# Early modulation sums and Hyena products moved to VectorE, the value transform folded modulo 4, and weight splits placed when both engines are empty

## The chip, the cores and the metric

The kernel runs on one core of a Trainium2 chip. The metric is the time of one execution on the device, in microseconds (us). In the text PE is TensorE, DVE is VectorE, ACT is ScalarE, POOL is GpSimd, and SP is the sync engine, whose queue issues nearly all transfers.

## What is computed

One inference step of a two-layer diffusion backbone for 512 latent tokens and 128 context tokens of width 1024 (640 columns in all). Layer 0 mixes attention and a long convolution (Hyena), layer 1 is a bidirectional mLSTM; after each comes a gated feed-forward part. Every part is shifted, scaled and gated by a modulation vector, once for the latents (`c`) and once for the context (`c_ctx`). The parts that the change touches:

```python
mod_p = jnp.split(silu(c_ctx) @ w_mod[l] + b_mod[l], 6, axis=-1)
mod_s = [m[:, None, :] for m in jnp.split(silu(c) @ w_mod[l] + b_mod[l], 6, axis=-1)]

def long_conv(v, h):                 # n = 2 L
    V = jnp.fft.rfft(v, n=n, axis=1)
    Hf = jnp.fft.rfft(h, n=n, axis=0)
    return jnp.fft.irfft(V * Hf[None], n=n, axis=1)[:, :L]

# Hyena: u -> x0, x1, v after a width-3 convolution
v = v * x1
y = long_conv(v, h_f) + flip(long_conv(flip(v), h_b)) + skip * v
return y * x0

# after each mixer
xp = xp + mod_p[2] * rms_norm(out_p, norm_mix_post[l])
xs = xs + mod_s[2] * rms_norm(out_s, norm_mix_post[l])
```

## The kernel before

**Products.** Weights come from memory in tiles of 128x1024 (512 KB, `wr`). Each is split into a rounded high part `wh` (an ACT cast) and a low part `wl` (a DVE subtraction), and so are the activations (`a0h`, `a0l`). A product is then the sum of three: high by high, high by low, low by high. The Hyena transforms and transposes run in plain fp32; each such matmul leaves two records in the trace, a transpose one.

**Order of the work.** A planner (`Order`) writes the program. It keeps an estimated clock for each engine. The main tasks are PE's, in a fixed sequence. Everything else (evacuations, modulation sections, the Hyena chain, attention) is a *side*: a generator that is stepped when its time has come by PE's clock (`pump`, lines 187 to 201). A side with a lead may start when DVE's and ACT's queues stand no more than that lead ahead of PE; one spawned with a slack is held to that slack instead. When no side is due and both queues are short, `pump` calls `idle`, which splits the next weights. PE executes in the order written, and so does every other engine: an instruction that waits holds up all behind it on its engine.

**A modulation section** (`mod_section`, one of six per layer, named by layer and number) multiplies 1024 rows of `w_mod` by the two vectors, in eight steps over tiles `mw` of 128x1024, of which two are resident. At each step the sum for the latents, `acc[0]`, is one DVE instruction (SCALAR_TENSOR_TENSOR). For the context ACT multiplies into `modp` and POOL adds it to `acc[1]`. Then PE sums over the partitions (`finish`): for sections (0,3) and (0,4) with one-column products `modt`, for the gate section (0,2) with products `modp` of `onesr` and the two parts of a split (`moda`, `modb`), whose result DVE multiplies by a gain row `modn` and stores in a row `gate`. Sections (0,3) and (0,4) run in the projection of layer 0. Section (0,2) is spawned with a slack once the four convolution outputs (keys `("y", i)`) are there; it lies around the start of attention, and its gates are needed by the first post-norm (`o0p0t`) at the end of the out-projection.

**Layer 0.** The up-projection `u` of the Hyena columns is convolved into `zh`; two of the three parts give the value `vx` (4 channel tiles). `gated_value` transposes each tile in four blocks of 128 times (`vxt`, `block`); block b holds every second time of one half. `long_conv` works in two halves of 256 channels: `forward` transforms with two frequency tiles, cosine and sine (4 matmuls of 256 columns each); DVE and POOL multiply by the filter's spectrum `gc`, `gs` (POOL takes one product of each pair); sums and differences give `ab`; `inverse` brings back each channel tile with 8 matmuls of 256 columns into `iy`, and a DVE instruction adds it to `vx`. The context has its own small transform (`vp`, `yp`, `iz`).

The projection of queries, keys and values (`qkv`) runs by token tile. `qkv_evac` evacuates one: ACT copies the value columns (`vv`), then the side yields until its keys are ready, then come the squares `qsq` for the norms, and the rotation. The keys are:

```python
nc.scalar.copy(at["v"][i], ps[:, 768:1024])
yield [("mod", 0, 3 + EARLY)] + [("qk", j) for j in range(i - 1)]
```

Attention follows: scores `s`, their maximum `mx` on DVE, the softmax `p`, transposes. `load_x` issues five loads of `x` (512 KB each) on SP once all tiles are evacuated. After the first feed-forward (`dn`, post-norm transposes `f0p0nt`) come the mLSTM's small columns and transposes (`colp`, `vT`).

All DVE, ACT and POOL instructions are recorded by one helper (line 278), all matmuls by another (359), all transposes by a third (370).

Of the kernel before, what the change touches and what calls it, by code (L numbers as in the profile page):

```python
# [18 lines left out]
P = 128  # L19
# [40 lines left out]
class Order:  # L60
# [10 lines left out]
    TIGHT = 4000.0  # L71

# [114 lines left out]
    def pump(self):  # L187
        while True:
            for s in self.sides:
# [130 lines left out]
def hybrid_step(ctx: ExitStack, tc: tile.TileContext, A: dict, O: dict):  # L320
# [158 lines left out]
    RB = 1  # L479
# [232 lines left out]
    def mod_section(l, s):  # L712

        def finish():
            yield
            if s not in (2, 5) and (l, s) in NOFOLD:
# [7 lines left out]
            if s not in (2, 5):  # L724
# [15 lines left out]
                return  # L740
            for g in range(2):
                t = row(f"gate{l}{s}{g}")
# [20 lines left out]
        w = [load(0)]  # L763
        acc = [row(f"acc{l}{s}{g}") for g in range(2)]
        prod = None
        if (l, s) in PAGES:
            prod = [(page(f"modp{l}{s}{n}")[:, 0:512], slice(n * 512, n * 512 + 512)) for n in range(2)]
        elif (l, s) not in WHOLE:
            prod = [(row(f"modp{l}{s}"), slice(0, D))]
        if s in (2, 5):  # L770
            bias = [page(f"modc{l}{s}{n}") for n in range(2)]
            for n in range(2):
                o = s * D + n * 512
                nc.sync.dma_start(bias[n][0:1, 0:512], A["b_mod"][l : l + 1, o : o + 512])
            gain = row(f"modn{l}{s}")
            src = A["post_mix" if s == 2 else "post_ffn"][l : l + 1, :]
            nc.sync.dma_start(gain, src.broadcast_to([P, D]))
        for k in range(KT):
# [25 lines left out]
    PAGES = ((0, 3), (0, 4))  # L804
    WHOLE = ()
    NOFOLD = ((0, 3), (0, 4))
    EARLY = 1
# [8 lines left out]
    SLACK0 = 4000.0  # L816
    SLACK1 = 1500.0
# [189 lines left out]
    def forward(ft, src_c, src_s, cols, C, S, name):  # L1007

        n = cols.stop - cols.start
        for comp, src, dst in ((0, src_c, C), (1, src_s, S)):  # L1010
            one = n <= 256
            yield "aux" if one else "mm"
            ps = (aux if one else mm)(f"{name}f{comp}")
            w = 256 if one else 512
            for par in range(2):
                for q in range(2):
                    o = (par * 2 + comp) * 256 + ft * P
                    MM(ps[:, par * w : par * w + n], hy["dft"][q][:, o : o + P],
                       src[par * 2 + q][:, cols], q == 0, q == 1)
            yield  # L1020
            t = page(f"{name}o{comp}")[:, 0:n]
            nc.scalar.copy(t, ps[:, w : w + n])
            nc.vector.tensor_tensor(dst[:, 0:n], ps[:, 0:n], t, op=ALU.add)
            if comp == 0:
                nc.vector.tensor_tensor(dst[:, n : 2 * n], ps[:, 0:n], t, op=ALU.subtract)
            else:
                nc.vector.scalar_tensor_tensor(dst[:, n : 2 * n], ps[:, 0:n], -1.0, t, op0=ALU.mult, op1=ALU.add)
            od.gave("aux" if one else "mm", ps)
            yield
# [51 lines left out]
    G = []  # L1081

    def filter_spectrum(ft):
        if ft < 2:
            gc, gs = row(f"gc{ft}"), row(f"gs{ft}")
            yield from forward(ft, hs, hd, slice(0, HC), gc, gs, f"g{ft}")
            G.append((gc, gs))
            return
        hy["gp"] = row("gp")
# [1011 lines left out]
```

## Time and profile before

| | |
|---|---|
| time, median of three runs | 1773.72 us (1772.31 to 1775.42) |
| the profiled execution | 1771.78 us, its span 1770.0 us, mean granted PE clock 0.984 |
| PE | 1702.6 us (96%), 10132 instructions |
| DVE | 1246.2 us (70%), 2035 |
| ACT | 765.3 us (43%), 1214 |
| POOL | 438.3 us (25%), 239 |
| moved by DMA | 203.87 MB, 115 GB/s on average |
| largest shares of the chain that ended last | PE 84%, DVE 9%, issue 3%, ACT 2% |

A share is that of an engine's busy time over the whole span; the stages differ. The chain that ended last is followed back from the last instruction to what released it. The idle time of an engine that is not the bound costs nothing. The page's slices show where PE is not full: at the start, and around 290 us.

### The profile page before, as it was taken

To read this page: it belongs to the slowest core of one execution; us is meant where nothing else is said; L and a number is where in the kernel's file an instruction comes from. 1 tells how busy PE (TensorE), PEld (TensorE's weight loads), DVE (VectorE), ACT (ScalarE), POOL (GpSimd) and SP (SyncE) were. 2 spreads that over 40 slices of the span, in tenths; PEclk is the share of its full clock that TensorE was granted. 3 is DMA by queue.
4 is the path that set the end of the run, shared out by engine and by line. 5 is a ranking of instruction groups with operands and counts; after the bars stand their busy time and mean duration, and the time that the engine had idled before them with its cause. 6 is when DMAs were issued, how large, how long until landed. Compare 5 with 4: busy or idle time off the path is not lost.

```text
span 1770.0 us, 25662 instructions
## 1 busy us (share of the span) xinstructions
PE 1702.6 (96%) x10132; PEld 1542.7 (87%) x10132; DVE 1246.2 (70%) x2035; ACT 765.3 (43%) x1214; POOL 438.3 (25%) x239
## 2 busy tenths in 40 slices
PE   7999898899999999999999999999989999999998
PEld 3598787689999999888789998999889999998886
DVE  5778797766878697886756888777468844445455
ACT  4544234654544344454555443335344433223343
POOL 0235423301455453440012211101014511111000
PEclk9999998999999999999999999999999999999999
DMA  7435143131434434463524311123114322223343
GB/s 272 152 134 164 60 131 113 38 106 49 155 132 158 136 136 143 136 209 109 180 98 143 117 54 50 54 71 110 62 38 173 109 76 72 72 84 105 122 158 128
DMA packets 63794, 203.87 MB, mean 115 GB/s; under 512 B 7159, under 2 KB 12279, under 8 KB 63674
## 3 DMA queue, kind: packets, MB, share of 16 engines
q1 hardware_dynamic: 63674, 202.23, 33.5%
q8 instruction: 80, 1.31, 0.3%
q14 instruction: 40, 0.33, 0.1%
HBM read 196.17 MB, written 3.94 MB: 113 GB/s over the span
## 4 chain that ended last, share of the span: by engine, by line
PE 84%; DVE 9%; issue 3%; ACT 2%; DMA 1%; POOL 1%; SPq 0%; DVEq 0%; ACTq 0%; POOLq 0%
PE u L359 20%; PE dn L359 17%; PE g L359 17%; PE o L359 6%; PE mk L359 3%; PE mo L359 3%; PE mq L359 3%; PE qkv L359 2%; PE mv L359 2%; DVE wl L278 1%; PE po L359 1%; PE mod L359 1%; PE modt L359 1%; PE s L359 1%; DVE qsq L278 1%
## 5 line engine op out<-in xcount | busy, mean ns | idle before, releaser
L278 DVE TENSOR_TENSOR wl<-wr,wh 128x1024 fp32r<-128x1024 f32 (+1 forms) x268 | 333.8, 1250 | 139.1 <-ACT wh L278 138.8
L278 ACT CAST wh<-wr 128x1024 fp32r<-128x1024 f32 (+1 forms) x268 | 272.2, 1019 | 173.5 <-PE dn L359 109.5
L278 POOL TENSOR_TENSOR acc<-acc,modp 128x1024 f32<-128x1024 f32 (+1 forms) x84 | 206.1, 2462 | 211.3 <-ACT modp L278 211.0
L278 POOL TENSOR_TENSOR hid<-zg,zu 128x640 f32<-128x640 f32 x44 | 106.1, 2411 | 324.4 <-DVE zu L278 314.1
L278 DVE SCALAR_TENSOR_TENSOR acc<-mw,sc,acc 128x1024 f32<-128x1024 f32 x70 | 152.1, 2172 | 4.2 <-DMA mw<-in_w_mod 3.8
L278 DVE SCALAR_TENSOR_TENSOR zg<-g,vec,zg 128x127 f32<-128x127 f32 (+3 forms) x168 | 87.4, 541 | 89.8 <-ACT zg L278 86.7
L359 PE MATMUL dn<-wh,hh 128*128 128x512 f32 x440 | 138.9, 396 | 1.1 <-DVE zu L278 1.1
L359 PE MATMUL dn<-wh,hl 128*128 128x512 f32 x440 | 138.3, 395 | 0.6 <-DVE hl L278 0.6
L359 PE MATMUL dn<-wl,hh 128*128 128x512 f32 x440 | 138.3, 394 | 0.0
L278 DVE SCALAR_TENSOR_TENSOR zu<-u,vec,zu 128x511 f32<-128x511 f32 (+2 forms) x164 | 86.7, 549 | 70.4 <-ACT zu L278 67.6
L278 ACT ACTIVATE modp<-mw,sc 128x1024 f32<-128x1024 f32 (+1 forms) x84 | 83.6, 1009 | 69.9 <-DMA mw<-in_w_mod 35.0
L359 PE MATMUL u<-a3h,wh 128*128 128x384 f32 (+1 forms) x336 | 105.6, 314 | 2.9 <-DVE a3h L278 2.9
L359 PE MATMUL u<-a3l,wh 128*128 128x384 f32 (+1 forms) x336 | 105.5, 314 | 1.5 <-POOL a3l L278 1.5
L359 PE MATMUL u<-a3h,wl 128*128 128x384 f32 (+1 forms) x336 | 105.2, 313 | 0.4 <-DVE wl L278 0.4
L359 PE MATMUL g<-a3h,wh 128*128 128x384 f32 (+1 forms) x336 | 104.9, 312 | 0.0
L359 PE MATMUL g<-a1h,wh 128*128 128x384 f32 (+1 forms) x336 | 104.8, 312 | 0.0
L359 PE MATMUL u<-a1h,wl 128*128 128x384 f32 (+1 forms) x336 | 104.3, 310 | 0.4 <-DVE wl L278 0.4
L359 PE MATMUL g<-a3l,wh 128*128 128x384 f32 (+1 forms) x336 | 104.6, 311 | 0.0
L359 PE MATMUL u<-a1l,wh 128*128 128x384 f32 (+1 forms) x336 | 104.1, 310 | 0.3 <-POOL a1l L278 0.3
L359 PE MATMUL g<-a3h,wl 128*128 128x384 f32 (+1 forms) x336 | 104.4, 311 | 0.0
L359 PE MATMUL u<-a1h,wh 128*128 128x384 f32 (+1 forms) x336 | 104.3, 310 | 0.0
L359 PE MATMUL g<-a1h,wl 128*128 128x384 f32 (+1 forms) x336 | 104.2, 310 | 0.0
(749 smaller groups left out, 4477.8 us busy)
## 6 DMA issues: line engine op xcount, KB each, us to landing
wr<-in_w_up SPq DMA_DIRECT2D x92, 512.0 KB
wr<-in_w_down SPq DMA_DIRECT2D x82, 512.0 KB
mw<-in_w_mod SPq DMA_DIRECT2D x80, 512.0 KB
wr<-in_w_ml SPq DMA_DIRECT2D x34, 512.0 KB
wr<-in_w_out SPq DMA_DIRECT2D x18, 512.0 KB
wr<-in_w_in SPq DMA_DIRECT2D x13, 512.0 KB
wr<-in_w_u SPq DMA_DIRECT2D x12, 512.0 KB
we<-in_w_mod SPq DMA_DIRECT2D x8, 512.0 KB
```

The source lines that it names most:

```text
L278: r = f(*args, **kw)
L359: r = nc.tensor.matmul(out, lhsT, rhs, start=start, stop=stop)
```

## The change

It has five parts.

1. In sections (0,3), (0,4) and (0,2) (`ALONE`) the context's sum is also one DVE instruction per step, behind a yield of its own. ACT's multiplication, POOL's addition and their pages are gone there.
2. The Hyena products that POOL did go to DVE (`HYE`). The rotation of queries and keys stays on POOL (`ROPE`).
3. The transform of the value is folded modulo 4: block b holds every fourth time. `forward` transforms with one tile of 128 frequencies for each block, and sums and differences on DVE make the four outputs of it; `inverse` has 8 matmuls of 128 columns per channel tile, from inputs `vx`, `vz` of 512 columns that DVE sums and subtracts first. The filter's spectrum is laid out by halves, and the gates replace `acc` in place of rows of their own. The gain row `modn` is loaded in `finish`, no longer at the section's start.
4. `pump` calls `idle` first when no urgent side waits and both DVE and ACT are behind PE. A buffer is released one step earlier (`RB`), and a lead of the feed-forward is smaller (`FLEAD`).
5. The evacuation of `qkv` no longer waits for section (0,4). Section (0,2) is spawned on the keys of (0,4) and of all five evacuated tiles, no longer on the convolution outputs.

```diff
@@ pump
+            if not self.urgent and max(self.t["DVE"], self.t["ACT"]) < self.clock + self.FIRST and self.idle():
+                continue
@@
-    RB = 1
+    RB = 0
@@ mod_section, finish
+            gain = row(f"modn{l}{s}")
+            src = A["post_mix" if s == 2 else "post_ffn"][l : l + 1, :]
+            nc.sync.dma_start(gain, src.broadcast_to([P, D]))
             for g in range(2):
-                t = row(f"gate{l}{s}{g}")
+                t = acc[g]
@@ mod_section, a step
                 nc.vector.scalar_tensor_tensor(acc[0], w[k], c[:, 0:1], acc[0], op0=ALU.mult, op1=ALU.add)
-                for t, a in prod or [(w[k], slice(0, D))]:
-                    nc.scalar.mul(t, w[k][:, a], c[:, 1:2])
-                    nc.gpsimd.tensor_tensor(acc[1][:, a], acc[1][:, a], t, op=ALU.add)
+                if alone:
+                    yield 0
+                    nc.vector.scalar_tensor_tensor(acc[1], w[k], c[:, 1:2], acc[1], op0=ALU.mult, op1=ALU.add)
+                else:
+                    nc.scalar.mul(prod, w[k], c[:, 1:2])
+                    nc.gpsimd.tensor_tensor(acc[1], acc[1], prod, op=ALU.add)
@@
+    ALONE = ((0, 3), (0, 4), (0, 2))
@@
+    HYE = nc.vector
+    ROPE = nc.gpsimd
@@ block
-        if b == 4:
-            return slice(LS, T)
-        t0 = (b // 2) + 2 * P * (b % 2)
-        return slice(t0, t0 + 2 * P - 1, 2)
+        return slice(LS, T) if b == 4 else slice(b, LS, 4)
@@ forward
+        for comp in range(2):
+            t = page(f"{name}t{comp}")[:, 0:512]
+            for n in (2, 0):
+                yield "aux"
+                ps = aux(f"{name}f{comp}{n}")
+                for q, c in enumerate((a, b)):
+                    o = ((n + q) * 2 + comp) * P
+                    MM(ps[:, c], hy["dft"][:, o : o + P], src[comp][n + q][:, cols])
+                if n:
+                    nc.scalar.copy(t, ps)
+                else:
+                    u = page(f"{name}u{comp}")[:, 0:512]
+                    nc.vector.tensor_tensor(u, ps, t, op=ALU.add)
+                    nc.vector.tensor_tensor(t, ps, t, op=ALU.subtract)
...
@@ inverse
-        for par in range(2):
-            for n, (ft, comp) in enumerate(((0, 0), (0, 1), (1, 0), (1, 1))):
-                o = ((2 if par else 2 * ft) + comp) * 256
-                MM(ps[:, par * 256 : par * 256 + 256],
-                   ab[par * 2 + comp][:, ft * 256 + cl : ft * 256 + cl + P],
-                   (hy["dft"][ft] if par else hy["dfi"])[:, o : o + 256], n == 0, n == 3)
+        for b in range(4):
+            for comp in range(2):
+                MM(ps[:, b * P : b * P + P], uv[b][:, comp * 256 + cl : comp * 256 + cl + P],
+                   hy["dfi"][:, (b * 2 + comp) * P : (b * 2 + comp) * P + P], comp == 0, comp == 1)
@@ long_conv
-            nc.gpsimd.tensor_tensor(two(m2), two(S), gs, op=ALU.mult)
+            HYE.tensor_tensor(x[1], S, gs, op=ALU.mult)
...
+        nc.vector.tensor_tensor(uv[0], p0, p1, op=ALU.add)
+        nc.vector.tensor_tensor(uv[2], p0, p1, op=ALU.subtract)
+        nc.vector.tensor_tensor(uv[1], m0, m1, op=ALU.add)
+        nc.vector.tensor_tensor(uv[3], m0, m1, op=ALU.subtract)
@@ qkv_evac
-        yield [("mod", 0, 3 + EARLY)] + [("qk", j) for j in range(i - 1)]
+        yield [("qk", j) for j in range(i - 1)]
@@
-    FLEAD = 1750.0
+    FLEAD = 1000.0
@@
-    tasks += [Task(begin_attn), spawn_mods(SLACK1, *[(0, 4), (0, 2)][EARLY:], keys=[("y", i) for i in range(4)])]
+    tasks += [Task(begin_attn), spawn_mods(SLACK1, *[(0, 4), (0, 2)][EARLY:], keys=[("mod", 0, 3 + EARLY)] + [("qk", i) for i in range(NTT)])]
```

On PE, at the first inverse of a channel tile, between two runs of projection products; before:

```order
L359 MATMUL qkv_0_1241<-wl_1393,a0h_557 128x512 x2
L359 MATMUL iy_1485<-dfi,ab_1167 128x256
L359 MATMUL iy_1485<-dfi,ab_1168 128x256
L359 MATMUL iy_1485<-dfi,ab_1167 128x256
L359 MATMUL iy_1485<-dfi,ab_1168 128x256
L359 MATMUL iy_1485<-dft_108,ab_1169 128x256
L359 MATMUL iy_1485<-dft_108,ab_1170 128x256
L359 MATMUL iy_1485<-dft_109,ab_1169 128x256
L359 MATMUL iy_1485<-dft_109,ab_1170 128x256
L359 MATMUL qkv_0_1241<-wh_1444,a0h_559 128x512 x2
```

and with the change:

```order
L362 MATMUL qkv_0_1229<-wl_1398,a0h_561 128x512 x2
L362 MATMUL iy_1449<-dfi,vx_1290 128x128 x2
L362 MATMUL iy_1449<-dfi,vz_1292 128x128 x2
L362 MATMUL iy_1449<-dfi,vx_1291 128x128 x2
L362 MATMUL iy_1449<-dfi,vz_1293 128x128 x2
L362 MATMUL qkv_0_1229<-wh_1431,a0h_563 128x512 x2
```

The inverse stands at the same place among the projection's products, with as many matmuls of half the columns.

On DVE, at the start of attention (`mx` is a row maximum of the scores, `modc` the bias of section (0,2), `zh` the last convolutions); before:

```order
L278 SCALAR_TENSOR_TENSOR zh_2228<-u_2175,vec,zh_2228 128x127 x2
L278 TENSOR_TENSOR acc_2096<-acc_2096,modc_2099 1x512
L278 TENSOR_TENSOR acc_2096<-acc_2096,modc_2100 1x512
L278 SCALAR_TENSOR_TENSOR acc_2096<-mw_2105,sc,acc_2096 128x1024
L278 TENSOR_REDUCE mx_2318<-s_2315 128x1
L278 TENSOR_SCALAR mx_2318<-mx_2318 128x1
L278 SCALAR_TENSOR_TENSOR zh_2325<-u_2234,vec,zh_2325 128x511 x2
```

and with the change:

```order
L281 TENSOR_SCALAR p_2267<-p_2267,rr_2264 128x640
L281 SCALAR_TENSOR_TENSOR zh_2314<-u_2177,vec,zh_2314 128x511 x2
L281 SCALAR_TENSOR_TENSOR zh_2314<-u_2177,vec,zh_2314 128x127 x2
L281 TENSOR_SCALAR acc_2364<-mw_2362,sc 128x1024
L281 TENSOR_REDUCE mx_2391<-s_2388 128x1
L281 TENSOR_SCALAR mx_2391<-mx_2391 128x1
L281 TENSOR_REDUCE mx_2401<-s_2398 128x1
```

The section's bias and accumulation leave their place ahead of the first maximum; its first multiplication (`acc<-mw`) now stands behind the softmax of early score tiles and ahead of the maxima of later ones.

On DVE, in the out-projection (`gate` or `acc` from `modp` are the gates, `o0l` the low parts of the projection's input); before:

```order
L278 TENSOR_TENSOR o0l_2875<-vx_820,o0h_2874 128x640
L278 TENSOR_TENSOR gate_2850<-modp_2880,modn_2103 128x512
L278 TENSOR_TENSOR wl_2900<-wr_1941,wh_2898 128x512
L278 TENSOR_TENSOR wl_2901<-wr_1941,wh_2899 128x512
L278 TENSOR_TENSOR o0l_2907<-vx_870,o0h_2906 128x640
L278 TENSOR_TENSOR wl_2914<-wr_2037,wh_2912 128x512
L278 TENSOR_TENSOR wl_2915<-wr_2037,wh_2913 128x512
L278 TENSOR_TENSOR o0l_2921<-vx_1039,o0h_2920 128x640
L278 TENSOR_TENSOR gate_2850<-modp_2933,modn_2103 128x512
L278 TENSOR_TENSOR modb_2939<-acc_2097,moda_2938 128x1024
```

and with the change:

```order
L281 TENSOR_TENSOR o0l_2973<-mx_2590,o0h_2972 128x640
L281 SCALAR_TENSOR_TENSOR acc_2364<-mw_2926,sc,acc_2364 128x1024
L281 SCALAR_TENSOR_TENSOR acc_2365<-mw_2926,sc,acc_2365 128x1024
L281 TENSOR_TENSOR modb_3013<-acc_2364,moda_3012 128x1024
L281 TENSOR_TENSOR acc_2364<-modp_3022,modn_3010 128x512
L281 TENSOR_TENSOR acc_2364<-modp_3032,modn_3010 128x512
L281 TENSOR_TENSOR modb_3037<-acc_2365,moda_3036 128x1024
L281 TENSOR_TENSOR acc_2365<-modp_3052,modn_3010 128x512
L281 TENSOR_TENSOR acc_2365<-modp_3062,modn_3010 128x512
L281 TENSOR_TENSOR o0p0t_3093<-o_0_2852,acc_2364 128x1024
```

The gates stood among the first products of the out-projection; now the section's last accumulations lie there, and both splits and all gates stand directly ahead of the first post-norm.

## Rows read from the trace of the kernel before

**Rows 1.** Windows: stretch, length, busy us (instructions) by engine, PEclk, DMA share, GB/s.

```profile
353.30:395.60 42.30, 42.30 (x184) 34.24 (x184) 25.36 (x41) 20.81 (x32) 0.00 (x0) 1.00 0.29 100
76.29:353.30 277.01, 249.74 (x1409) 218.50 (x1409) 220.40 (x351) 122.24 (x241) 103.32 (x63) 0.95 0.32 108
```

**Rows 2.** Timeline of PE: start, duration, operation; x8 counts records.

```profile
161.17 1.89 PE L359 MATMUL v10f<-vt,dft 128*128 128x256 f32 x8
162.71 0.59 PE L359 MATMUL qkv<-wh,a0h 128*128 128x512 f32 x1
...
191.26 1.89 PE L359 MATMUL iy<-dfi,ab 128*128 128x256 f32 x8
...
194.52 0.82 PE L359 MATMUL qkv<-wh,a0h 128*128 128x512 f32 x2
...
201.60 3.63 PE L359 MATMUL modt<-ones,acc 128*128 128x1 f32 x32
```

**Rows 3.** Waits of PE, 76.29 to 284.5 us: total, times, longest.

```profile
PE qkv L359 <- DVE qsq L278: 3.4, 2, 2.2
...
PE u L359 <- DVE qsq L278: 2.8, 1, 2.8
PE iy L359 <- DVE ab L278: 2.7, 2, 2.1
```

**Rows 4.** Timeline of ACT, 184 to 215 us.

```profile
188.22 0.37 ACT L278 COPY vv<-qkv 128x256 f32<-128x256 f32 x1 [7.65 <-PE qkv L359]
...
205.05 1.51 ACT L278 ACTIVATE qsq<-qkv 128x768 f32<-128x768 f32 x2 [2.65 <-PE modt L359]
```

**Rows 5.** Tile acc, 100 to 204 us: min/median/max ns, first and last start.

```profile
L278 POOL TENSOR_TENSOR acc<-acc,modp x28: 1257/1510/2349, 101.3 to 201.0; 128x512 f32<-128x512 f32 x28
L278 DVE SCALAR_TENSOR_TENSOR acc<-mw,sc,acc x14: 1270/1534/2348, 103.1 to 196.4; 128x1024 f32<-128x1024 f32 x14
```

**Rows 6.** Groups of DVE, 130 to 270 us: count, busy us, mean ns, idle before.

```profile
L278 DVE TENSOR_TENSOR vc<-vc,gs 128x512 f32<-128x512 f32 x4 | 5.7, 1418 | 0.1
L278 DVE SCALAR_TENSOR_TENSOR vx<-vx,vec,iy 128x512 f32<-128x512 f32 x4 | 3.0, 738 | 2.0 <-PE iy L359 2.0
```

**Rows 7.** Groups of DVE by form, 284.5 to 353.3 us.

```profile
L278 DVE TENSOR_TENSOR wl<-wr,wh 128x512 fp32r<-128x512 f32 x2 | 1.3, 684 | 0.0
```

**Rows 8.** Timeline of DVE, 281 to 299 us.

```profile
281.13 4.69 DVE L278 TENSOR_TENSOR acc<-acc,modc 1x512 f32<-1x512 f32 x2
...
285.86 2.45 DVE L278 SCALAR_TENSOR_TENSOR acc<-mw,sc,acc 128x1024 f32<-128x1024 f32 x1
...
288.23 0.81 DVE L278 TENSOR_REDUCE mx<-s 128x1 f32<-128x640 f32 x1
```

**Rows 9.** Timeline of PE, 286.5 to 300 us; in brackets the idle time before and releaser.

```profile
291.54 2.08 PE L359 MATMUL s<-qkT,qkT 128*128 128x512 f32 x2 [4.72 <-ACT p L278]
```

**Rows 10.** Windows at half clock, columns as in rows 1, and one of the transfers.

```profile
290.48:300.72 10.24, 8.46 (x25) 5.75 (x26) 7.99 (x18) 6.01 (x15) 0.00 (x0) 0.50 0.71 284
945.84:952.66 6.82, 6.82 (x34) 6.08 (x32) 4.35 (x8) 3.22 (x5) 0.00 (x0) 0.50 0.80 311
290.00:294.00 4.00, 2.46 (x4) 1.18 (x4) 1.67 (x3) 2.25 (x4) 0.00 (x0) 0.56 0.97 382
```

**Rows 11.** Waits of PE, 880 to 960 us.

```profile
PE colp L370 <- DVE wi L278: 1.9, 1, 1.9
PE vT L370 <- ACT mvs L278: 1.7, 1, 1.7
```

**Rows 12.** Timeline of DVE, 380 to 400 us.

```profile
381.17 1.23 DVE L278 TENSOR_TENSOR o0p0t<-o,gate 128x1024 f32<-128x1024 f32 x1 [10.38 <-ACT o0p0j L278]
```

**Rows 13.** Timeline of SP, 279 to 302 us: the loads of x are issued.

```profile
288.81 2.40 SPq L278 DMA_DIRECT2D x<-in_x  x5
```

**Rows 14.** Timeline of PE, 112 to 161 us: four transposes of a value tile.

```profile
114.87 0.63 PE L370 MATMUL vxt<-ident,vx 128*128 128x128 f32 x4
```

More of the change, by code (lines that the diff above doesn't have):

```diff
@@ L763, in mod_section @@
         w = [load(0)]
+        alone = (l, s) in ALONE
         acc = [row(f"acc{l}{s}{g}") for g in range(2)]
[L765 to L769, printed above, removed]
+        if not alone:
+            prod = row(f"modp{l}{s}")
         if s in (2, 5):
@@ L1079, in load_win, with filter_spectrum @@
             nc.sync.dma_start(hy["win"][b][:, 0:HC], A["hy_win"][b])
[L1081 to L1087, printed above, removed]
+    G = {}
+    def filter_spectrum(n):
+        if n < 2:
+            w = 512
+            for comp, src in enumerate((hs, hd)):
+                yield "mm"
+                ps = mm(f"g{n}f{comp}")
+                for par in range(2):
+                    for q in range(2):
+                        b = 2 * q + par
+                        o = (b * 2 + comp) * P
+                        MM(ps[:, par * w : par * w + w], hy["dfg"][n][:, o : o + P], src[b][:, 0:HC], q == 0, q == 1)
+                yield
+                t = page(f"g{n}o{comp}")[:, 0:HC]
+                g = row(f"g{n}{'cs'[comp]}")
+                two = g.rearrange("p (h a c) -> p h a c", h=2, a=2)
+                half = lambda x: x.rearrange("p (h c) -> p h c", h=2)
+                nc.scalar.copy(t, ps[:, w : 2 * w])
+                nc.vector.tensor_tensor(two[:, :, 0], half(ps[:, 0:w]), half(t), op=ALU.add)
+                if comp == 0:
+                    nc.vector.tensor_tensor(two[:, :, 1], half(ps[:, 0:w]), half(t), op=ALU.subtract)
+                else:
+                    nc.vector.tensor_tensor(two[:, :, 1], half(t), half(ps[:, 0:w]), op=ALU.subtract)
+                od.gave("mm", ps)
+                for hf in range(2):
+                    G[hf, n, comp] = g[:, hf * 512 : hf * 512 + 512]
+                yield
             return
-        hy["gp"] = row("gp")
+        hy["gp"] = [page(f"gp{q}")[:, 0:512] for q in range(2)]
         yield "mm"
@@ new lines, in long_conv @@
+        yield from forward((vt, vt), cols, cs, f"v{hf}")
+        x, z = ([page(f"v{n}{q}{hf}")[:, 0:512] for q in range(2)] for n in "xz")
+        sd = []
+        for n in range(2):
+            (C, S), (gc, gs) = cs[2 * n : 2 * n + 2], (G[hf, n, c] for c in range(2))
+            nc.vector.tensor_tensor(x[0], C, gc, op=ALU.mult)
+            HYE.tensor_tensor(x[1], S, gs, op=ALU.mult)
+            nc.vector.tensor_tensor(C, C, gs, op=ALU.mult)
+            HYE.tensor_tensor(S, S, gc, op=ALU.mult)
+            nc.vector.tensor_tensor(x[0], x[0], x[1], op=ALU.subtract)
@@ L1894, in hybrid_step @@
     hy["z"], hy["w"], hy["w3"] = page("hyz"), page("hyw"), row("hyw3")
-    hy["dft"] = [row(f"dft{q}") for q in range(2)]
+    hy["dfg"] = [row(f"dft{q}") for q in range(2)]
+    hy["dft"] = hy["dfg"][0]
     hy["dfp"] = page("dftp")
```

119 lines of the change are left out of this document (51 added, 68 removed).

## The prediction

> **What bounds the kernel now.** I read first the busy shares by stage, then the waits of TensorE (PE), then the timelines at each place where the change puts something else, and last the orders of the two programs. Over the span PE is nearly always busy, and PE's order is the same in both programs up to shortly before the Hyena transforms. So time can come from two sources only: PE work that disappears, and PE idle or half-clock time that disappears. Most of the change lies between 76 and 353 us, the Hyena, projection and attention stages. There PE is busy 249.74 of 277.01 us, VectorE (DVE) 220.40, and GpSimd (POOL) 103.32 [rows 1]. The reader should see that PE is still the longest engine there, but that DVE with 80% has only 56.6 us of room. In the out-projection (353.30 to 395.60) PE has no idle time at all [rows 1]: whatever comes too late there costs its full length.
>
> **The change, part by part.** The sum is made against the profiled execution, 1771.78 us (span 1770.0), which lies 1.94 under the median of the three runs; I take the difference from the median, 1773.72.
>
> A, the shorter transform. In the forward direction one piece of four matmuls runs from 161.17 to the next product at 162.71, so 1.54 us [rows 2]; there are 8 pieces (two halves, two frequency tiles, cosine and sine), 12.3 us. The change keeps 8 matmuls of the 16 per half, with the same 256 columns. In the inverse direction a channel tile runs from 191.26 to 194.52, 3.26 us [rows 2]; four tiles, 13.0. There the count of 8 matmuls stays and their columns go from 256 to 128. Half of 25.3 is 12.7. One thing speaks against the full half of the inverse: a product of a single column still takes 3.63/32 = 0.113 us for each of its records, since the weights must be loaded [rows 2]. The 16 records of an inverse tile then take at least 1.8 instead of 1.63, 0.2 us in each of four tiles less than the half, so A lies between −11.9 and −12.7. I take −12.5, all of it on PE, which is the path here.
>
> B, the projection's evacuation. PE waits 3.4 us for qsq, the squares of the query and key columns [rows 3]. Their tile left PE early: ScalarE copied its value columns at 188.22, but squared the rest at 205.05 only, right behind modt, the last product of modulation section (0,4) [rows 4]. The reason is a key in the evacuation that waits for that section, and the change takes the key out. What is late next is the tile's own evacuation chain, 17 us earlier and beside two tiles of projection. I take the whole −3.4; bounds 0 and −3.4.
>
> C, DVE waits in the projection. u waits 2.8 us for qsq and iy 2.7 us for ab [rows 3]. Both are DVE being late. DVE loses the POOL competition (below) but gains work, so I take half, −2.8; bounds 0 and −5.5.
>
> DVE's account decides whether A to C arrive. Added: 14 accumulations for the context vector at 1.27 (the fastest of the same instruction, [rows 5]) = 17.8; 8 products of 512 at 0.684, the price of a two-operand instruction of 512 elements without company [rows 7], and 4 products of 256 at no more than that = 8.2; in the folded transform 8 additions of 512 per half that were not there = 16 × 0.684 = 10.9. Together 36.9 us. Taken away: DVE instructions that run beside POOL are slow now. The rows that I can count are 14 accumulations at a median of 1.534 instead of 1.27 (3.7 us, [rows 5]), four products at 1.418 instead of 0.684 (2.9, [rows 6]), and two bias additions at 4.69 instead of 1.37 and one accumulation at 2.45 instead of 1.27 (3.3 + 1.2, [rows 8]): 11.1 in all. POOL loses its 28 accumulations of 1.51 us, 42.3 of its 103.32 [rows 1, 5], and its products too, so more rows than these gain; I take twice the counted, 22, and keep 0 and 30 as ends. DVE then has 220.4 + 36.9 − 22 = 235.3 us to do in 277.0 − 24.1 = 252.9 (A to D): 93%. That is full but possible.
>
> D, the start of attention. PE waits 4.72 us before the score product at 291.54 [rows 9], for p, the softmax, which waits for the row maximum at 288.23, which stands on DVE behind the bias additions and an accumulation of section (0,2) [rows 8]. [...] In the changed order (0,2) no longer stands in front of the first score; its accumulations follow the early score tiles. So 8.9 us go. But section (0,2) now stands between score tiles: DVE's first instruction on its weights, a multiplication, is queued ahead of the maxima of the next tiles, and behind it waits all of the softmax, and PE behind that. Its weight tile is issued behind the two cache outputs and the five loads of x on the sync engine's (SP) queue. In the program of before these five loads go out at 288.81 [rows 13] and the stretch that follows moves 382 GB/s [rows 10]; their 2.6 MB with the 0.5 MB of the weight tile are an estimated 8.1 us at that rate. If the slack of the four tiles hides all of this, the wait is 0; if nothing hides it, it is some 7. I take 3.5, the middle, as no row shows how far DVE has come then. D is −5.4, bounds −1.9 and −8.9.
>
> E, behind the first feed-forward. PE waits 1.9 and 1.7 us for the small mLSTM columns [rows 11], and then 6.82 us pass at half clock, 3.4 lost [rows 10]. The changed order spreads the boundary's transposes to within 12 products of the end of the down-projection (before, the last of this tile stood 96 ahead), and takes the column work later. That moves the same work, so I take 3.0 of the 7.0; bounds +1 and −7.0.
>
> F, section (0,2) ends later. Its last 8 accumulations, about 8 × 1.28 us, and two splits now lie in the out-projection, where PE has no slack. PE's first gate product now stands 96 products into it; at 42.30/184 = 0.23 us each [rows 1] that is 22 us, and DVE's instructions ahead of the split, counted in the changed order at the durations above, sum to an estimated 23. DVE idles 10.38 us there before the first post-norm [rows 12], so a small lateness is hidden. The gain row now leaves SP's queue behind three up-projection loads, early enough. I take +2.0; bounds 0 and +6.
>
> The strided access. The value transposes, four of which run 0.63 us, read every second element now [rows 14], and every fourth after; the skip additions of 512 elements, 0.738 each [rows 6], gather from two PSUM pieces now and four after. I take no change, as no row shows a step of four. [...] No run here shows that step. If such reads took twice as long, 16 transposes add 16 × 0.16 = 2.5 us on PE and four additions 3.0 on DVE, at most 5.5: the sum would be −19.6 instead of −25.1.
>
> The remaining edits (weight splits when both queues are empty, earlier release of one buffer, a smaller lead) cost no instruction; what they move is in D, E and F.
>
> Sum: −12.5 − 3.4 − 2.8 − 5.4 − 3.0 + 2.0 = −25.1 us. The median becomes 1773.7 − 25.1 = 1748.6.
>
> **Rivals.** *Stride.* [...] Chance 0.11.
>
> *DVE becomes the bound.* If POOL's departure gives DVE nothing back, DVE has 220.4 + 36.9 = 257.3 us to do in the stretch. At the 93% of my account this takes 276.7, as long as now; only E and F are left, −1, and the time is 1772.7. Against it speak the 11.1 us of counted slow rows. Chance 0.08.
>
> *Section (0,2) comes too late, and it is slower.* The place is the end of attention. If DVE does all of the 16 accumulations (20.3 us) and two splits (2.5) after the softmax work, with the 8.1 us of loads in front and a half-clock stretch behind as at 290 us (4.2), the gates come 35.1 us late and PE, which works in order, stands. With the 5.5 for the new waits in D and F taken out this is 1748.6 − 5.5 + 35.1 = 1778.2. It decides from about 34 us of lateness. For it speaks that only two weight tiles are resident and each turns round through DVE; against it that the order puts 8 of the 16 before the out-projection. Chance 0.07.
>
> **How the numbers follow.** The forecast has the remaining 0.74. Its own range: all gains without cost are 12.7 + 3.4 + 5.5 + 8.9 + 7.0 = 37.5, 1736.2, and the runs scatter 1.4 below their median, so 1734; upwards the least A, half of B and the upper costs (−11.9 − 1.7 − 1.9 + 6) give −9.5, 1764. The range 1734 to 1766 holds the forecast and the stride case, and leaves out the last two rivals and the tails. A measurement can tell about 0.2% (3.5 us) from no change. Faster: forecast, stride and a quarter of the DVE case, 0.87; same: the rest of it, 0.06; slower: 0.07.
>
> **What would show it.** A: an inverse tile of about 1.7 us and half as many forward records. B: the qsq squares right behind their tile's copy. C and DVE: no accumulation much over 1.3 us, and DVE at about 93% from 76 us to the end of attention. D: no pause and no half clock at the first scores; a DVE wait for mw in its place is the new cost. E: the half-clock stretch at 946 gone or shorter. F: PE without a wait for the gates in the out-projection. The forecast is wrong if DVE's mean durations stay (no relief), or if PE stands for acc or modb.

## The result and the profile after

The changed kernel takes 1747.53 us (median of 4 runs, 1745.86 to 1750.14), the kernel before, beside it, 1774.38; the ratio is 0.9852, 95% interval 0.9840 to 0.9864. Run again later it took 1747.23 us, ratio 0.9846 (0.9819 to 0.9872). The profiled execution has 1745.86 us with a span of 1744.0, 26.0 less than before. The forecast of 1748.6 us is met within 1.1 us. It was not met stage by stage, so that part of this is luck, and the runs show that its terms do not simply add.

The windows of the changed kernel, columns as in [rows 1]: from the first up-projection to the out-projection, the out-projection, and the stage behind the first down-projection. The first two answer to [rows 1]; the third follows a stage that before ran from 892.55 to 958.27, 65.72 us.

```profile
76.03:334.25 258.22, 228.32 (x1375) 203.43 (x1375) 217.35 (x393) 95.71 (x201) 21.07 (x16) 0.96 0.33 110
334.25:394.55 60.30, 60.30 (x275) 48.83 (x274) 47.15 (x77) 30.62 (x48) 3.06 (x3) 1.00 0.35 123
873.30:932.85 59.55, 56.17 (x398) 54.79 (x397) 42.21 (x80) 37.19 (x62) 8.77 (x17) 1.00 0.36 114
```

The first stretch has lost 18.8 us, the out-projection (59.8 us before) gained 0.5, the stage behind the down-projection lost 6.2; the rest of the program together 1.5. POOL went from 103.32 us in the stretch to 21.07, and DVE, with 42 instructions more (393 instead of 351; the prediction put them at an estimated 36.9 us), has 217.35 instead of 220.40.

The transform, on the timeline of PE (start, duration, operation), answers to [rows 2]. An inverse tile takes from 172.61 to 174.50, 1.89 us where it took 3.26; its 16 records cost 0.118 each, and a product of one column 0.113 [rows 2]. A piece of the forward transform, half as long as before, takes from 205.47 to 206.14:

```profile
172.61 0.61 PE L362 MATMUL iy<-dfi,vx 128*128 128x128 f32 x4
...
174.50 0.71 PE L362 MATMUL qkv<-wh,a0h 128*128 128x512 f32 x2
...
205.47 1.03 PE L362 MATMUL v1f<-vt,dft 128*128 128x256 f32 x4
206.14 0.82 PE L362 MATMUL qkv<-wh,a0h 128*128 128x512 f32 x2
```

The waits of PE from 70 to 275 us (total, times, longest) answer to [rows 3]. The wait for ab, now for the sums in vx and vz, is gone, but the waits for qsq are 13.5 us instead of 6.2:

```profile
PE u L362 <- DVE qsq L281: 8.7, 1, 8.7
PE qkv L362 <- DVE qsq L281: 4.8, 1, 4.8
```

The timeline of ACT (bracket: idle time before and what ended it) answers to [rows 4]. The squares of the first tile do stand right behind the copy of its values. The squares of the third tile, however, come at 230.29, behind the transposes of earlier tiles:

```profile
178.03 0.37 ACT L281 COPY vv<-qkv 128x256 f32<-128x256 f32 x1 [6.36 <-PE qkv L362]
178.30 0.82 ACT L281 ACTIVATE qsq<-qkv 128x768 f32<-128x768 f32 x1
...
230.29 0.87 ACT L281 ACTIVATE qsq<-qkv 128x768 f32<-128x768 f32 x1
```

On DVE four accumulations stand between the first tile's last step and the second tile's reduction (190.64), and PE waits behind them; its product at 195.16 says so. The two timelines:

```profile
183.20 0.96 DVE L281 TENSOR_TENSOR qsq<-qkv,qn0y 128x768 f32<-128x768 f32 x1
184.07 0.34 DVE L281 SCALAR_TENSOR_TENSOR vx<-vx,vec,iz 128x128 f32<-128x128 f32 x1
184.33 4.87 DVE L281 SCALAR_TENSOR_TENSOR acc<-mw,sc,acc 128x1024 f32<-128x1024 f32 x4
...
190.64 0.94 DVE L281 TENSOR_REDUCE qss<-qsq 128x6 f32<-128x768 f32 x1
```

```profile
195.16 1.19 PE L362 MATMUL qkv<-wh,a0h 128*128 128x512 f32 x2 [4.77 <-DVE qsq L281]
...
238.20 0.66 PE L362 MATMUL u<-a0h,wh 128*128 128x384 f32 x1 [8.72 <-DVE qsq L281]
```

Tile acc from 100 to 215 us (min/median/max ns) answers to [rows 5]: 28 accumulations, none over 1.283 us, where 14 had a median of 1.534 and a worst case of 2.348.

```profile
L281 DVE SCALAR_TENSOR_TENSOR acc<-mw,sc,acc x28: 1271/1278/1283, 102.1 to 205.8; 128x1024 f32<-128x1024 f32 x28
```

### The profile page after: what moved, and what is told of

It is laid out like the page before. It is cut to its first block, busy times and chain, and to the rows that moved or that the text cites. A ratio compares the mean times of both kernels' runs of the same rounds, so it can differ in the third digit from the quotient of the medians.

```text
span 1744.0 us, 25540 instructions
## 1 busy us (share of the span) xinstructions
PE 1675.4 (96%) x10100; PEld 1525.1 (87%) x10100; DVE 1253.9 (72%) x2084; ACT 740.5 (42%) x1176; POOL 358.6 (21%) x192
## 4 chain that ended last, share of the span: by engine, by line
PE 85%; DVE 10%; ACT 2%; issue 2%; DMA 0%; POOL 0%; SPq 0%; DVEq 0%; ACTq 0%; POOLq 0%
PE u L362 19%; PE dn L362 17%; PE g L362 17%; PE o L362 6%; PE mk L362 3%; PE mq L362 3%; PE mo L362 3%; PE mv L362 2%; PE qkv L362 2%; DVE wl L281 2%; PE po L362 1%; PE modt L362 1%; DVE acc L281 1%; PE s L362 1%; PE mod L362 1%
## 5 line engine op out<-in xcount | busy, mean ns | idle before, releaser
L281 POOL TENSOR_TENSOR acc<-acc,modp 128x1024 f32<-128x1024 f32 x49 | 144.9, 2957 | 113.1 <-ACT modp L281 112.8
L281 DVE SCALAR_TENSOR_TENSOR acc<-mw,sc,acc 128x1024 f32<-128x1024 f32 x91 | 164.3, 1819 | 1.6 <-DMA mw<-in_w_mod 1.2
L281 ACT ACTIVATE zu<-u,vec 128x640 f32<-128x640 f32 (+1 forms) x42 | 36.8, 875 | 161.0 <-PE u L362 160.9
L362 PE MATMUL g<-a1l,wh 128*128 128x384 f32 (+1 forms) x336 | 104.2, 310 | 0.0
```

Of the source, the lines that this page charges most:

```text
L281: r = f(*args, **kw)
L362: r = nc.tensor.matmul(out, lhsT, rhs, start=start, stop=stop)
```

## The experiments

Each kernel is the changed one with one edit, or the one before with a part of the change. To compare them, the table takes the stretch from the first up-projection to the out-projection apart: its length, PE's idle time in it, and what half clock cost, worked out in slices of 0.2 us as PE's busy time times one minus the granted clock. What is left is PE's work at full clock. The kernel before, run beside each group of them, had medians of 1772.5 to 1775.1 us. How far such numbers repeat can be read from four profiles: changed, changed again, old_release and release_only execute the same instructions in the same order on PE, DVE, ACT and POOL up to 418 us. Their stretch took 258.1 to 260.1 us, with 27.4 to 30.0 us of idle time and 7.4 to 12.9 lost at half clock. Differences no larger than these, of 2, 3 and 5 us, can belong to the execution. A profile is also one execution only: those of pool_sums and no_fold are the fastest of their kernels' executions, those of fold_only and no_qk_key the slowest.

| kernel | time, us (ratio to before, 95%) | stretch | idle | lost at half clock | PE work |
|---|---|---|---|---|---|
| before | 1774.4 | 277.0 | 27.3 | 13.8 | 236.0 |
| changed | 1747.5 (0.9852, 0.9840 to 0.9864) | 258.2 | 29.9 | 7.5 | 220.8 |
| changed, again | 1747.2 (0.9846, 0.9819 to 0.9872) | 258.1 | 27.4 | 10.3 | 220.4 |
| fold_only | 1791.4 (1.0103, 1.0086 to 1.0119) | 288.5 | 42.5 | 20.1 | 225.9 |
| no_fold | 1756.3 (0.9899, 0.9882 to 0.9917) | 265.7 | 18.7 | 13.0 | 233.9 |
| pool_sums | 1771.5 (0.9985, 0.9971 to 1.0000) | 275.2 | 36.8 | 16.4 | 222.0 |
| pool_products | 1772.8 (0.9994, 0.9984 to 1.0004) | 276.7 | 37.1 | 18.9 | 220.6 |
| old_key | 1766.3 (0.9967, 0.9956 to 0.9977) | 276.6 | 36.8 | 17.0 | 222.7 |
| old_start | 1757.7 (0.9915, 0.9898 to 0.9933) | 261.5 | 29.0 | 11.7 | 220.8 |
| old_release | 1757.3 (0.9910, 0.9894 to 0.9926) | 260.1 | 27.5 | 12.9 | 219.8 |
| release_only | 1759.0 (0.9911, 0.9884 to 0.9938) | 258.2 | 30.0 | 7.4 | 220.9 |
| no_qk_key | 1751.7 (0.9875, 0.9856 to 0.9893) | 265.4 | 25.8 | 19.7 | 219.8 |
| fewer_ahead | 1764.4 (0.9945, 0.9925 to 0.9965) | 270.6 | 35.4 | 14.8 | 220.3 |
| none_ahead | 1770.4 (0.9977, 0.9964 to 0.9991) | 264.3 | 30.0 | 12.6 | 221.7 |

The repeat of the changed kernel:

> The changed kernel once more, beside these. Its first four runs lie between 1745.9 and 1750.1 us; expected 1746 to 1750 us, with the waits of PE for qsq of 4.8 and 8.7 us at their place if they belong to the order, and with half-clock stretches at other places if those are a matter of the run.

Its waits for qsq stand where they stood, 4.8 and 9.5 us (one more of 0.6): they belong to the order. The stage behind the down-projection took 61.1 instead of 59.6 us and the start before the first up-projection 77.6 instead of 76.0, with the same idle time or less and more half clock: those belong to the run.

**The fold alone, and all but the fold.** In fold_only everything else is as before, but for the gates that replace `acc` and the later load of their gain row, which no_fold has too:

```diff
-    HYE = nc.vector
+    HYE = nc.gpsimd
-    ALONE = ((0, 3), (0, 4), (0, 2))
+    ALONE = ()
-        yield [("qk", j) for j in range(i - 1)]
+        yield [("mod", 0, 3 + EARLY)] + [("qk", j) for j in range(i - 1)]
```

(and the pump, the start of (0,2), RB and FLEAD as before)

> The kernel before with the value transform folded modulo 4 and nothing else of the change: context sums on ACT and POOL, Hyena products on POOL, the evacuation's key, the start of section (0,2), the buffer release and the lead as before. Theory 'PE work is the path': what TensorE no longer multiplies comes out in full, 4 x 1.37 us in the inverse and 8 x 0.85 us in the forward direction, 12.3 us: about 1762 us, with VectorE's extra additions absorbed. Rival 'VectorE takes it back': 16 more additions of 512 elements, beside POOL at up to 1.4 us each (11 to 23 us), stand in front of what PE waits for, and most of the gain is eaten: 1768 to 1774 us.

It is 17.6 us slower than before; both theories missed. In the profiles the stretch is 11.5 us longer, and the mLSTM 6.4 us (274.3 instead of 267.9): there PE waits 7.8 us for hs, of which the fold computes nothing. The planner has written another order there, as it has in pool_sums, old_start and release_only, where the same wait is 5.7 us. So of the 17.6 us only the stretch's part tells of the fold. The waits of PE in the stretch, and two windows, the stretch and a part of it:

```profile
PE qkv L360 <- DVE wl L279: 6.9, 4, 2.5
PE vpp L360 <- DVE vx L279: 6.5, 1, 6.5
...
PE u L360 <- DVE zh L279: 4.0, 2, 2.8
PE iy L360 <- DVE vx L279: 3.6, 1, 3.6
PE s L360 <- DVE qsq L279: 3.1, 1, 3.1
```

```profile
78.05:366.55 288.50, 246.01 (x1378) 212.61 (x1379) 226.83 (x368) 121.52 (x238) 103.11 (x63) 0.92 0.31 104
...
198.40:222.40 24.00, 16.82 (x54) 13.68 (x54) 12.85 (x38) 4.62 (x7) 8.54 (x6) 0.50 0.04 14
```

PE has ten microseconds of work less and 15.2 more idle time, and for 24 us in one piece its granted clock is 0.50. DVE is busy for 226.83 of 288.50 us, 79%: it is not full. PE waits since the piece that it needs stands late in DVE's queue, and DVE's pieces are long while POOL runs: its product of vf and g0s takes 1.180 us here and 0.678 in the changed kernel (groups of DVE, mean ns before the second bar's idle time):

```profile
L279 DVE TENSOR_TENSOR vf<-vf,g0s 128x512 f32<-128x512 f32 x2 | 2.4, 1180 | 0.1
```

```profile
L281 DVE TENSOR_TENSOR vf<-vf,g0s 128x512 f32<-128x512 f32 x2 | 1.4, 678 | 0.0
```

no_fold is the other half: the kernel before with all the rest of the change.

```diff
-        nc.gpsimd.tensor_tensor(two(m2), two(S), gs, op=ALU.mult)
+        nc.vector.tensor_tensor(two(m2), two(S), gs, op=ALU.mult)
+    ALONE = ((0, 3), (0, 4), (0, 2))
```

(likewise the other Hyena products, the keys, RB, FLEAD, the gates in place)

> Everything of the change but the folded transform: context sums and Hyena products on VectorE, the gates in place, the key, the start of section (0,2), the release and the lead as changed; the transform as before. Theory 'POOL's departure is the condition': without POOL beside it VectorE has room, PE keeps its 12.3 us of transform, VectorE saves 10.9 us of additions: about 1747.5 + 12 = 1758 to 1762 us, so that most of the 26 us come without the fold. Rival 'the fold is the gain': moving sums and products to VectorE alone is worth nothing, and the time is that of before, 1768 to 1774 us.

'POOL's departure' holds in its main point: 16 us of the 27 by the medians, 18 by the ratio, come without the fold, some 2 us more than the expected range allowed. But the key, the start of (0,2), the release and the lead are in this kernel too, and no run has the moves to VectorE alone. Its stretch has the least idle time of all kernels, 18.7 us; its row:

```profile
73.85:339.50 265.65, 246.93 (x1406) 218.23 (x1407) 212.90 (x377) 96.33 (x205) 23.41 (x16) 0.95 0.32 107
```

The fold then takes 13.1 us of PE work out (233.9 against 220.8) and gives 5.7 back as idle time and half clock (31.8 against 37.4): the stretch becomes 7.4 us shorter, the kernel 8.8 us faster. In fold_only, where POOL still works beside DVE and the key, the start and the release are those of before, the same fold makes the stretch 11.5 us longer.

**Each of the two moves to VectorE undone.**

```diff
-    ALONE = ((0, 3), (0, 4), (0, 2))
+    ALONE = ((0, 2),)
+    PAGES = ((0, 3), (0, 4))
```

> The changed kernel with the context sums of sections (0,3) and (0,4) back on ACT and POOL (section (0,2) stays on VectorE alone). Theory 'relief': with POOL adding beside it VectorE's accumulations go from 1.28 back to about 1.5 us and its other instructions slow down too, so the evacuations come later although VectorE has 14 instructions fewer; 1752 to 1758 us. Rival 'queue order': PE's waits for qsq (4.8 and 8.7 us in the changed kernel) come of accumulations standing ahead of the evacuation on VectorE, half as many of them shorten the waits: 1742 to 1747 us.

```diff
-    HYE = nc.vector
+    HYE = nc.gpsimd
```

> The changed kernel with its Hyena products (8 of 512 and 4 of 256 elements) back on POOL. Theory 'relief': each product on POOL holds up VectorE's neighbour and the chain of the transform, 8 x about 0.7 us on VectorE given back but about as much lost to slower neighbours; PE does not wait for the inverse's input (no such wait is left), so 1746 to 1750 us. Rival 'chain': the transform comes later, PE waits for it as it waited 2.7 us for ab before: 1750 to 1753 us.

Either one alone takes nearly the whole gain away, 24 and 25 us; 'relief' named the direction of the first and far too little of it, and nothing expected the size of the second. In the profile of pool_sums 17.0 us stand in the stretch and 4.4 in the mLSTM, at the wait for hs. In pool_products twelve products cost 18.4 us of the stretch. The windows of pool_products, its stretch and a part of it, and its timelines of DVE and of POOL, where additions of 256 elements take 1.50 us and end 0.3 us behind POOL's products, and 0.41 directly after:

```profile
77.01:353.67 276.66, 239.56 (x1374) 212.86 (x1375) 221.35 (x379) 95.79 (x201) 41.07 (x28) 0.92 0.30 100
...
230.00:310.00 80.00, 63.15 (x346) 57.91 (x347) 61.23 (x121) 19.78 (x48) 20.28 (x14) 0.79 0.21 76
```

```profile
238.33 1.50 DVE L281 TENSOR_TENSOR vp<-vx 128x256 f32<-128x256 f32 x1
239.76 1.50 DVE L281 TENSOR_TENSOR vp<-vf 128x256 f32<-128x256 f32 x1
241.19 0.41 DVE L281 TENSOR_TENSOR vm<-vx 128x256 f32<-128x256 f32 x1
```

```profile
237.90 1.66 POOL L281 TENSOR_TENSOR vx<-vf,g1s 128x512 f32<-128x512 f32 x1 [4.37 <-DVE vx L281]
239.63 1.35 POOL L281 TENSOR_TENSOR vf<-vf,g1c 128x512 f32<-128x512 f32 x1
```

DVE is busy for 80% of this stretch. Of the 18.4 us, 7.2 are idle time of PE and 11.4 half clock. The edit also moves other work, since the planner reckons with POOL's times; slower neighbours and order are not told apart here. Both are there: summed over DVE's instructions in the stretch, what each took beyond the shortest of the same names and shape in any of the fourteen traces is 19.6 us here and 7.7 in the changed kernel.

**The keys of the evacuation.**

```diff
-        yield [("qk", j) for j in range(i - 1)]
+        yield [("mod", 0, 3 + EARLY)] + [("qk", j) for j in range(i - 1)]
```

> The changed kernel with the evacuation of qkv waiting for section (0,4) again. Theory B of the prediction: the squares of the first two tiles come behind modt again and PE's waits for qsq grow: 1750 to 1753 us. Rival: the changed kernel waits for qsq longer than the one before (13.5 us against 6.2), since the chain behind the squares is what is late, so the key is worth nothing: 1744 to 1748 us.

Direction B, at more than five times its price: 18.8 us. With the sums on DVE the key binds two chains together, and PE waits in front of both ends. Slower neighbours explain little of it: DVE's time beyond the shortest is 11.6 us, against 7.7 in the changed kernel. The waits of PE from 76 to 420 us:

```profile
PE modt L362 <- DVE acc L281: 6.3, 2, 5.7
PE qkt L373 <- DVE qsq L281: 5.4, 1, 5.4
PE qkv L362 <- DVE qsq L281: 4.8, 2, 3.7
```

```diff
-        yield [("qk", j) for j in range(i - 1)]
+        yield
```

> The changed kernel with the last key of the evacuation taken out too: a tile's squares no longer wait for the transposes of the tile two before it. In the changed kernel PE waits 8.7 us for qsq at 238 us; its tile's squares stood on ACT behind those transposes and three weight casts. Theory 'the key is late': the wait mostly goes and a half-clock stretch with it, 1736 to 1743 us. Rival 'VectorE is full': the wait moves to another place on VectorE, 1745 to 1750 us.

The wait of 8.7 us is gone, and others come in its place (u for zh 6.6 instead of 2.8, qkv for wl 3.2 instead of 1.6): this is the rival's direction, though the time is 1.7 us above its range. The profile says less than it seems to. Its stretch is 7.2 us longer, with 4.1 us less idle time and 12.2 more lost at half clock. But up to 220 us the two programs have the same instructions in the same order on all four engines, and there 3.5 of the 7.2 us, 2.1 of the 4.1 and 6.5 of the 12.2 stand already: they belong to the execution. Taking the wait away has won nothing; whether the kernel has become slower stays open, as the two intervals overlap.

**The accumulations in front of the evacuation.**

```diff
-    SLACK0 = 4000.0
+    SLACK0 = 2000.0
```

> The changed kernel with the slack of sections (0,3) and (0,4) at 2000 instead of 4000 ns (SLACK0): an accumulation is placed only when VectorE's queue is shorter, so between the evacuations of the first two query-key tiles stand 2 accumulations instead of 4, the others follow later, some beside the last up-projection. Theory 'accumulations ahead': they cause the 4.8 us wait for qsq at 195 us, which shrinks by about the 2.5 us that two of them take, with part of the half clock behind it: 1741 to 1745 us. Rival: every place on VectorE up to the attention is as full, the accumulations hold up another evacuation: 1747 to 1753 us.

```diff
-    SLACK0 = 4000.0
+    SLACK0 = 1000.0
```

> The same with the slack at 1000 ns: no accumulation between the two evacuations, and section (0,4) ends in the attention. Theory 'accumulations ahead': the 4.8 us wait goes but for a rest, 1738 to 1744 us. Rival: VectorE is as full later, and section (0,2), which starts after (0,4), comes too late for the first post-norm of the out-projection, so that PE stands there: 1752 to 1765 us.

In both the wait at 195 us does shrink, qkv for qsq from 4.8 to 2.3 and 1.2 us, so the accumulations cause it; and both are slower, by 17 and 23 us, more than their rivals said. In fewer_ahead the same work stands in front of other steps (u waits 10.9 us for qsq and 6.8 for zh, where it waited 8.7 and 2.8). In none_ahead the mechanism of the prediction's slower rival shows itself: section (0,2) comes too late, PE stands for it in the out-projection, and the stage takes 77.41 instead of 60.30 us. Waits of PE from 341 to 420 us, and the window:

```profile
PE modp L362 <- ACT moda L281: 4.3, 1, 4.3
PE o L362 <- DVE o0p0t L281: 2.0, 1, 2.0
...
PE modp L362 <- DVE acc L281: 0.8, 1, 0.8
```

```profile
341.95:419.36 77.41, 67.83 (x274) 52.38 (x275) 63.60 (x93) 29.20 (x43) 6.64 (x6) 0.87 0.40 136
```

**The start of section (0,2).**

```diff
-    tasks += [Task(begin_attn), spawn_mods(SLACK1, *[(0, 4), (0, 2)][EARLY:], keys=[("mod", 0, 3 + EARLY)] + [("qk", i) for i in range(NTT)])]
+    tasks += [Task(begin_attn), spawn_mods(SLACK1, *[(0, 4), (0, 2)][EARLY:], keys=[("y", i) for i in range(4)])]
```

> The changed kernel with section (0,2) started on the four convolution outputs again. Theory D: bias and accumulation stand in front of the first row maximum again, PE pauses about 5 us and runs at half clock behind it (4.2 us lost): 1754 to 1758 us. Rival: without POOL beside them the two bias additions take 1.4 instead of 4.7 us and the accumulation 1.3 instead of 2.5, so the pause is short whatever the order: 1746 to 1750 us.

The total agrees with theory D, the place does not. The stretch is only 3.3 us longer, all of it behind 265 us, where the orders part (1.4 us of idle time, 1.7 at half clock), with no pause of 5 us, as the rival has it; 5.3 us come from the mLSTM (272.9 us instead of 267.6), where PE waits once for hs. The waits of PE from 960 to 1230 us:

```profile
PE hT L373 <- DVE hs L281: 5.7, 1, 5.7
```

The edit touches nothing there; the planner, whose clocks run on from the attention, has written another order.

**The release and the lead.**

```diff
-    RB = 0
+    RB = 1
-    FLEAD = 1000.0
+    FLEAD = 1750.0
```

> The changed kernel with the buffer release (RB) and the feed-forward's lead (FLEAD) of before: the transposes behind the first feed-forward and the small mLSTM columns stand in the old order. Theory 'boundary order': from the end of the first down-projection to the first mq the stage takes 65.7 us again instead of 59.6, with the waits for colp and vT and the half clock at its place, and the total is about 1753.5 us. Rival 'chance of the clock': the half-clock stretch there has nothing to do with the order; the waits alone return, 2 us, and the total is 1748 to 1750 us.

```diff
-    RB = 0
+    RB = 1
```

> The changed kernel with the buffer release (RB) of before and the new lead (FLEAD). The transposes behind the first feed-forward stay in the new, spread order, while the small mLSTM columns (vT, colp) go back to the old. Theory 'columns': the stage behind the down-projection takes 65 us again, since the waits for colp and vT and the half clock behind them hang on the columns: 1753 to 1757 us. Rival 'transposes': the spread of the transposes is what helps, the stage stays at 60 to 61 us: 1747 to 1750 us.

'Boundary order' and 'columns' hold for the stage. It takes 65.74 and 65.83 us, as before the change, with the old waits (of old_release, 877 to 943 us; in release_only they are 1.2 and 2.4 us), and the release alone does it:

```profile
PE colp L373 <- DVE wi L281: 1.9, 1, 1.9
PE vT L373 <- ACT mvs L281: 1.7, 1, 1.7
```

The totals are 3.8 and 2 us above the top of what was expected. Release_only has the same 5.7 us wait for hs in the mLSTM. In the profile of old_release 2.9 us stand ahead of the out-projection, where its order is still that of the changed kernel, so they belong to the execution; the feed-forward ahead of the stage and the mLSTM behind it are 1.0 and 1.1 us longer. The lead alone was not run; with the release of before it made no difference to the stage.

The last part of the change, the line in `pump`, needs no run: without it the planner writes the same instructions in the same order on all engines, so here it does nothing.

## Why the prediction was right, point by point

**A held as a term, not as a gain.** Forecast −12.5; by the rows above the inverse lost 4 × 1.37 = 5.5 us and the forward direction 12.3 − 8 × 0.67 = 6.9, together 12.4. But in the kernel before it would have cost time (fold_only, 11.5 us in the stretch), and in the changed one its worth is 7.4 us of the stretch.

**B failed in sign, for the waits.** It said that what is late next is the tile's own chain, and took that as free. That chain was longer than the wait it replaced: the second tile's reduction stands behind four accumulations (every second one is new on DVE by part 1), and the third tile's squares behind two tiles' transposes. PE's waits for qsq went from 6.2 to 13.5 us, 7.3 more, where B and C together forecast 6.2 less for these and iy. The 2.7 us for the inverse's input did go. And taking the key out is worth 18.8 us once the sums are on DVE, not 3.4, for with the key the evacuation waits for them.

**DVE's account was mis-sized and asked the wrong question.** I took 22 us of relief, with 30 as the upper end. At its face value it was 220.4 + 36.9 − 217.4 = 39.9 us (section (0,2)'s own pieces changed places too). Instruction by instruction, DVE's time in the stretch beyond the shortest of the same names and shape was 42.0 us before, 40.8 of it in instructions that overlap one of POOL's, and is 7.7 now: 34.3 us of relief. DVE is at 84%, not 93%. But in the kernels whose stretch is long it is at 79 to 81%: its fullness does not decide. In fold_only, pool_sums and pool_products DVE's pieces are slower (38.1, 29.5 and 19.6 us beyond the shortest); in old_key and fewer_ahead (11.6 and 10.9) they hardly are, and what is left is which piece stands in front of the one that PE waits for. The rival 'DVE becomes the bound' describes the outcome of three of the experiments, 1766 to 1773 us, by the wrong mechanism.

**D was too careful.** Forecast −5.4. Its 8.9 us were the wait of 4.72 [rows 9] and 4.2, half of the 8.46 us for which PE was busy at a granted clock of 0.50 [rows 10]. The waits of 4.7 and 0.6 us at the first scores have become 0.5, there is no half clock at that place (the granted clock is 1.00 from 280 to 334.25 us), and no wait for section (0,2)'s weights. So the whole 8.9 came and the 3.5 of new wait did not. By old_start the new place accounts for 3.3 us. No run isolates the rest; in old_start DVE's two bias additions take 2.7 us where they took 4.7.

**E was the right place and half the size.** Forecast −3.0, measured −6.2 in the first profile and −4.6 in the second. The waits for colp are gone (those for vT are 3.1 us instead of 1.7). Of the 3.4 us lost at half clock there none is left in the first profile, 1.7 in the second. The cause is the earlier release, by release_only.

**F** was +2.0 and measured +0.5. The mechanism that it priced exists (none_ahead), but had room here.

**The sum.** A to D were to bring 24.1 us and brought 18.8; E and F brought 6.2 − 0.5 = 5.7 instead of 1.0; the rest of the program brought 1.5 that nothing had forecast. So the median came out right by luck: an error of 5.3 met one of 4.7 and a small remainder. Part of the first 18.8 is the clock: idle time rose by 2.6 us and half clock fell by 6.2, of which only the 4.2 at the first scores was in the forecast; in the other three profiles of the same order half clock was 7.4 to 12.9 us, so the size of this part belongs to the execution. The range held and its rivals were the right ones, but a chance of 0.74 for such a sum was bold: five edits that had a few microseconds each in the sum, or none, cost 10 to 25 when undone one at a time, 88 together, where the whole change brought 27. Some of that is order that the planner wrote anew elsewhere (the wait for hs).

**Stride.** It costs nothing here: four transposes at a step of four elements take 0.64 us against 0.63 at a step of two [rows 14], and the skip additions 0.738 as before [rows 6]. The skip additions read their SBUF operand in order in both kernels and gather from PSUM alone, in two pieces before and in four now. That reads at the longer step could take twice as long, 2.5 us on PE and 3.0 on DVE, was the prediction's assumption; no run shows it. The transposes on the timeline of PE of the changed kernel:

```profile
148.94 0.64 PE L373 MATMUL vxt<-ident,vx 128*128 128x128 f32 x4
```

## What to carry to other kernels

When a change has several parts on the same engine's queue, price them together: here the fold alone cost 17.6 us, all the rest without it brought 16 to 18, and both brought 27. Ask for each piece that the bounding engine waits for what will stand in front of it in its queue, not how full that engine is. And before you read a difference between two profiles, look where the two programs begin to differ: what differs ahead of that place belongs to the execution. Here the loss at half clock alone came out between 7.4 and 12.9 us for one order.

## What the runs showed of the hardware

POOL beside DVE cost more than expected: 28 accumulations on DVE at a median of 1.278 us with POOL nearly quiet (1.94 us busy from 100 to 215 us), 14 at a median of 1.534 and up to 2.348 with POOL adding (55.27 us busy from 100 to 204); additions of 256 elements at 1.50 instead of 0.41, over 0.3 us after POOL's product was. An addition of 0.41 us thus took 1.09 more while a product ran on POOL (pool_products); what causes it, no run shows. Taking 82 us of POOL's work away left DVE, with 42 instructions more, busy for 3 us less.

Two stretches at a granted clock of 0.51 stand at the two longest pauses of PE between the first up-projection and the out-projection of the changed kernel. A pause of 4.77 us lasts until 195.16, and in its last part 6.9 us at that clock begin; one of 8.72 us lasts until 238.20 and overlaps with 7.0 us at it (windows, columns as in [rows 1]):

```profile
193.50:200.40 6.90, 5.24 (x13) 4.18 (x14) 6.80 (x12) 0.60 (x2) 0.00 (x0) 0.51 0.25 73
234.40:241.40 7.00, 3.20 (x10) 3.23 (x11) 6.66 (x19) 0.00 (x0) 0.00 (x0) 0.51 0.38 136
```

The second lies half inside the pause and costs 1.6 us of PE's 3.20, the first 2.6 of 5.24. But the same order does not always meet the same clock. In the four profiles of one order the stretch took 258.2, 258.1, 258.2 and 260.1 us, with 29.9, 27.4, 30.0 and 27.5 us of idle time and 7.5, 10.3, 7.4 and 12.9 lost at half clock (changed, again, release_only, old_release). In the second a shorter idle time made up for the clock, in the last it did so only in part.

A plain fp32 matmul of 128 columns took 0.118 us per record and one of a single column 0.113 [rows 2], so 127 columns more cost 0.005. The weight loads of the 32 records of a single column took about as long as the products themselves, 3.76 us or 0.118 each (timeline of PEld of the kernel before):

```profile
201.39 3.76 PEld L359 LDWEIGHTS modt<-ones,acc 128*128 128x128 f32 x32
```
